# A two-layer encoder with a mixture of experts: the last tile's router products ahead of the other tiles' counts and gathers, and one copy of the gathered rows

## The chip, the cores and the metric

The kernel runs on one core of a Trainium2 chip. The time is the device time of one execution in microseconds (us), as a median of runs.

## What is computed

The reference is an encoder of two layers over 512 tokens of 1024 features in fp32. Each layer is a mixer (layer 0: retention and differential attention; layer 1: latent attention and gated linear attention), a residual and a layer norm, then a mixture of experts, another residual and another layer norm. The part that the change touches is the way from the mixer's output to the first expert, the router:

```python
grp_logits = xf @ w_grp + b_grp                 # 4 groups
g_idx = argmax(grp_logits)                      # top-1 group
exp_logits = (xf @ w_exp + b_exp).reshape(n, 4, 8)
in_grp = exp_logits of the chosen group         # 8 experts
top_l, top_e = lax.top_k(in_grp, 2)             # top-2 experts
gate = p_grp * softmax(top_l)
out = sum over the two experts e: gate * (silu(x @ w_gate[e]) * (x @ w_up[e])) @ w_down[e]
x = layer_norm(ALPHA * x + out)
```

There are 32 experts, each with three matrices of 2 MB, so a layer reads 201 MB of expert weights.

## The kernel before, in words

The 512 tokens are four tiles t = 0 to 3 of 128 rows. At the end of each layer's mixer, `out_rest` multiplies the last tiles by the output weights and routes all four. Its TensorE (PE) and VectorE (DVE) work runs in the order in which it is written, since `manual_schedule` names both engines there. ScalarE (ACT) and GpSimd (POOL) work is ordered by the scheduler.

The steps of a tile t are small helpers within `out_rest`:

- `total(t)` and `norm(t)`: the residual and the layer norm on DVE, and the tile's store to `x1d` in DRAM.
- `turn(t)`: eight 128x128 transposes on PE into PSUM, which two ACT copies bring to `mxT` (L1004).
- `logits(t)`: eight products of `mxT` with the 36 router columns.
- `choose(t)`: thirteen DVE steps that pick the group and the two experts, as closures in a list that `moe_choose` returns. The last one writes the 0/1 matrix `rab` (L1037).
- `count(t)`: 32-column products of `rab` with a triangle (`tri`) and, for the tiles ahead of it, with `ones`. They number the tokens of each expert. A tile's count needs the choices of all tiles up to it.
- `place(t)`: two DVE steps, `rpos` (L1048) and `S` (L1052). `S` is a 0/1 matrix that says which token goes to which of 64 places of the first experts.
- `gather(t)`: two products of 512 columns that add the rows of tile t, picked by `S`, to `m["g"]` in PSUM (tile name `pb`).

After the last tile, `moe_fit` finds out whether any expert has over 64 tokens and writes `rover`. All five engines then load `rover` (L1293), compare it and branch (L1294) over a slow general path that isn't taken here. In `moe`, the gathered rows `m["g"]` are copied to SBUF, one half by ACT and one by DVE (L1300). They are transposed on PE and copied by ACT (L1141), and the first expert's products `up(0, 0)` begin: 64 rows by 512 columns, in the rows `pa<-big 128*64 128x512`.

Expert weights come as 1 MB loads on SP's queue, in the order in which they are used. A load is issued as soon as a buffer slot is free, and slots come free as PE uses up earlier loads. SP takes the branch too, so loads that stand behind it in its queue wait for `rover`.

Of the kernel before, what the change touches and what calls it, by code (L numbers as in the profile page):

```python
# [77 lines left out]
class Kernel:  # L78
# [372 lines left out]
    def out_rest(self, pool, gbuf, m):  # L451

        nc = self.nc
        res = [self.residual(m, t) for t in range(NT)]
        first, last = self.order[:2], self.order[2:]
        ps, xT = {}, {}

        def begin(t):
            self.out_open(t)
            for q in first:  # L460
                self.out_mm(t, (2 * q, 2 * q + 1), q == first[0], False)

        def half_room():

            self.spare += 3
            for q in first:
                self.free(*self.out_w[q])
            self.free(*self.catbuf.pop(self.order[0] // 2))
            m.update(xbuf=self.slot(), xr=self.slot(), sc=self.slot(F32R))
            m["S"] = m["sc"][:, 0:D].rearrange("p (t e n) -> p t e n", t=NT, n=CAP)  # L470
            self.nc.gpsimd.memset(self.moe_fetched(m, 1), 0.0)
            self.spare -= 3
            self.pump()

        def out(t, *qs):
            for q in qs or last:
                if q not in self.out_w:
                    self.out_w[q] = self.next_w()
                self.out_mm(t, (2 * q, 2 * q + 1), False, q == last[-1])

        def room():

            for q in last:
                self.free(*self.out_w[q])
            self.free(*self.catbuf.popitem()[1])

        def total(t):

            tiles, halves = self.out_ps.pop(t)
            w = D // len(tiles)  # L490
            for i, z in enumerate(tiles):
                x = res[t][:, i * w:(i + 1) * w]
                nc.vector.scalar_tensor_tensor(x, x, ALPHA, z, op0=OP.mult, op1=OP.add)
            self.rel(*tiles)
            return self.ln_stats(pool, res[t])

        def norm(t, st):
            self.ln_apply(res[t], st, gbuf)
            nc.scalar.dma_start(self.x1d[t * P:(t + 1) * P, :], res[t])

        def turn(t):
            if t < 2:
                ps[t] = [self.pb()]
                halves = [ps[t][0][:, 0:512], ps[t][0][:, 512:D]]
            else:
                halves = ps[t] = [self.pa(), self.pa()]
            xT[t] = pool.tile([P, D], F32, name="mxT", bufs=3).rearrange("p (j n) -> p j n", j=KJ)
            self.moe_turn(m, xT[t], res[t], halves)

        def logits(t):  # L510

            z = ps[t]
            self.moe_logits(m, xT[t], z[0][:, 0:36])
            ps[t] = z, z[0][:, 0:36], (z[0][:, 512:D] if len(z) == 1 else z[1])[:, 0:NE]

        def choose(*ts):
            for steps in zip(*[self.moe_choose(m, pool, t, ps[t][1]) for t in ts]):
                for f in steps:
                    f()

        def count(t):
            self.moe_count(m, t, ps[t][2])

        def place(t, n=2):
            self.moe_place(m, t, ps[t][2], 2 * n)
            self.rel(*ps[t][0])

        def gather(t):

            if t == 0:  # L530
                m["g"] = self.pb()
            S = m["S"][:, t, 0:2].bitcast(F32).rearrange("p e n -> p (e n)")
            for hf in range(2):
                s = slice(hf * 512, (hf + 1) * 512)
                self.mm(m["g"][:, s], S, res[t][:, s], t == 0, t == NT - 1)

        while len(self.split_ready) < 2:
            self.prep_w()
        with self.tc.manual_schedule(engines={mybir.EngineType.PE, mybir.EngineType.DVE}):
            begin(2)  # L540
            begin(3)
            half_room()
            out(0)
            norm(0, total(0))
            out(1)
            norm(1, total(1))
            out(2)
            turn(0)
            norm(2, total(2))
            out(3, last[0])  # L550
            logits(0)
            choose(0)
            turn(1)
            out(3, last[1])
            room()
            count(0)
            st = total(3)
            place(0)
            logits(1)
            norm(3, st)  # L560
            turn(2)
            gather(0)
            logits(2)
            turn(3)
            choose(1, 2)
            count(1)
            place(1)
            logits(3)
            gather(1)
            count(2)  # L570
            place(2)
            choose(3)
            gather(2)
            count(3)
            place(3, 1)
            self.moe_fit(m)
            gather(3)
            self.moe_slots(m, 3, 2, 2)
# [623 lines left out]
    def moe(self, m, g, b):  # L1202

        nc, tc, l = self.nc, self.tc, m["layer"]
# [56 lines left out]
        def up(e, c):  # L1261
            if c == 0:
                acc[e] = self.pa()
            self.moe_up(acc[e], xn[:, e // 2 % 2, :, e % 2 * CAP:(e % 2 + 1) * CAP], c)
            if c == 1:
                h[e] = hh[64:128]
                self.moe_hidden(h[e], acc.pop(e))
# [27 lines left out]
            self.moe_general(m, r)  # L1295
        with tc.manual_schedule(engines={mybir.EngineType.PE}):
            x = self.moe_fetched(m, 0)
            for hf in range(2):
                s = slice(hf * 512, (hf + 1) * 512)
                (nc.scalar.copy, nc.vector.tensor_copy)[hf](x[:, s], m["g"][:, s])  # L1300
            self.rel(m.pop("g"))
            self.moe_features(x, xn[:, 0], 2)
            ps = self.pa()
            self.moe_tokens(m, m["S"][:, :, 2:4], self.idr, ps, 1)
            self.rel(ps)
            self.moe_fetch(m, 1, False)
            self.moe_gates(m)
            self.spare = 1
            up(0, 0)
            yhl = self.slot(F32R)  # L1310
            self.spare = 0
            up(0, 1)
            up(1, 0)
            for e in range(NE):
                q, k = divmod(e, 4)
                p = e // 2 - 1
                if e == NE - 10:
                    self.spare = 4
                if e == NE - 8:
                    last, cz, yz, gbuf = self.slot(local=False), self.slot(F32R, local=False), self.slot(F32R, local=False), None  # L1320
                    gbuf = self.load_gb(g, b)
                    self.spare = 0
                    nc.vector.tensor_copy(cz[:, T:T + P], self.eye)
                if e:
                    up(e, 1)
                    down(e - 1)
                    if e + 1 < NE:
                        up(e + 1, 0)
                if e == NE - 1:
                    hidden(e)  # L1330
                    break
                if e == 0:
                    features(1)
                    pair(0), pair(1)
                more = q + 1 < NE // 4
                if k % 2:
                    hidden(e)
                    if more and k == 1:
                        pair(2 * q + 3)
                    elif more:  # L1340
                        features(2 * q + 3)
                    continue
                add = 0 <= p < LAST - 1
                if add:
                    sums(p, 0)
                hidden(e)
                if add:
                    sums(p, 1)
                if more and k == 0:
                    pair(2 * q + 2)  # L1350
                elif more:
                    features(2 * q + 2)
                if add:
                    sums(p, 2, 3)
                if p == LAST - 2:
                    self.spare = 1
                    self.free(sc, yhl)
                    y = yz.rearrange("p (k n) -> p k n", k=2)
                    parts(0)
                    self.spare = 2  # L1360
                if e == NE - 2:
                    self.spare = 0
                    parts(1), parts(2)
            y1 = last[:, 0:D]
            sum_begin(0)
            down(NE - 1)
            sum_begin(1)
            for t in range(3):
                sum_end(t)
                if t == 0:  # L1370
                    sum_begin(2)
# [559 lines left out]
```

## Time and profile before

| | us |
|---|---|
| median of 3 runs (lowest, highest) | 1568.62 (1567.82, 1569.14) |
| the profiled execution: its time | 1568.2 |
| the profiled execution: its span, from the first to the last instruction | 1566.4 |
| PE busy | 1495.4 (95%) |
| DVE busy, ACT busy | 688.4 (44%), 441.1 (28%) |
| DMA queue of the weight loads | 69.8% of 16 engines' span |

PE is busy nearly everywhere, but not at one pace: the granted clock says in which stretches it ran at its lower level. Between the output products and the experts, PE, DVE and ACT hand small pieces to each other. There the timeline has to be read instruction by instruction.

### The profile page before, as it was taken

What the parts mean: (1) busy time and instruction counts of PE and PEld (TensorE: products, weight loads), DVE (VectorE), ACT (ScalarE), POOL (GpSimd) and SP (SyncE); (2) the same over time, 40 slices, a digit from 0 to 9 for tenths busy, and PEclk for the clock granted to TensorE, in tenths of its full rate; (3) what the DMA queues carried; (4) which work ended last, traced back from release to release, by engine and by line L of the source; (5) the groups of instructions that cost most, each with busy time, mean ns of one, the idle gap of its engine ahead of it and who ended that gap; (6) DMA issues with size and microseconds to landing.
All of it is one profiled execution on the core that took longest, in us unless ns stands there. A gap on an engine that the chain in (4) does not pass through costs nothing. (4 is left out here: it accounts for less than half of the span.)

```text
span 1566.4 us, 19698 instructions
## 1 busy us (share of the span) xinstructions
PE 1495.4 (95%) x7825; PEld 892.1 (57%) x7825; DVE 688.4 (44%) x1211; ACT 441.1 (28%) x772; POOL 185.7 (12%) x278
## 2 busy tenths in 40 slices
PE   7999999979999999999999899997999999999997
PEld 7888888844444444444358687675444444444433
DVE  4555655543334334343445634365333434334334
ACT  4545522012121121121235534512222122121222
POOL 3322211211000000010022200020100000001001
PEclk9999999989999999999999999999999999999998
DMA  8311133669999999999972111286999999999993
GB/s 239 109 54 54 55 108 134 243 236 393 425 426 426 426 427 425 426 426 426 427 260 97 54 54 55 79 340 261 401 426 427 425 427 427 425 426 425 427 427 127
DMA packets 106836, 465.11 MB, mean 297 GB/s; under 512 B 12972, under 2 KB 48268, under 8 KB 57456
## 3 DMA queue, kind: packets, MB, share of 16 engines
q1 hardware_dynamic: 98848, 444.86, 69.8%
q0 software_dynamic: 6160, 12.62, 2.3%
q10 hardware_dynamic: 1728, 6.29, 1.0%
q8 instruction: 63, 1.03, 0.2%
q14 instruction: 37, 0.30, 0.1%
HBM read 462.11 MB, written 9.44 MB: 301 GB/s over the span
## 5 line engine op out<-in xcount | busy, mean ns | idle before, releaser
L213 PE MATMUL pa<-big 128*64 128x512 f32 (+3 forms) x4168 | 831.0, 459 | 7.1 <-DMA big<-in_moe_w_up_dram 2.9
L213 PEld LDWEIGHTS pa<-big 128*128 128x128 f32 (+1 forms) x4168 | 449.5, 166 | 314.4 <-issue 268.1
L213 PE MATMUL pa<-big,hs 128*64 128x512 f32 x992 | 224.7, 592 | 0.0
L1198 DVE SCALAR_TENSOR_TENSOR big<-pa,rgate,big 64x512 fp32r<-64x512 f32 x120 | 90.0, 750 | 213.4 <-ACT big L1197 213.2
L213 PE MATMUL pb<-big 128*128 128x512 f32 (+1 forms) x544 | 160.3, 432 | 9.1 <-DVE big L1153 4.2
L1153 DVE SCALAR_TENSOR_TENSOR big<-big,pb 128x1024 f32<-128x1024 f32 x112 | 134.2, 1219 | 69.8 <-PE pb L213 69.5
L213 PEld LDWEIGHTS pa<-big,hs 128*64 128x64 f32 x992 | 72.9, 137 | 140.6 <-issue 136.0
L1197 ACT ACTIVATE big<-pa,rgate 64x512 fp32r<-64x512 f32 x120 | 81.8, 682 | 219.1 <-PE pa L213 170.3
L1168 DVE TENSOR_TENSOR h<-pa,h 64x512 f32<-64x512 f32 x64 | 44.5, 695 | 218.9 <-ACT h L1167 218.9
L213 PEld LDWEIGHTS pb<-big 128*128 128x128 f32 x544 | 98.0, 190 | 53.4 <-issue 25.2
L1167 ACT ACTIVATE h<-pa 64x512 f32<-64x512 f32 x64 | 37.6, 588 | 264.0 <-PE pa L213 264.0
L203 DVE TENSOR_TENSOR big<-big 128x2048 fp32r<-128x2048 f32 (+2 forms) x38 | 77.2, 2032 | 64.6 <-ACT big L203 46.6
L203 ACT CAST big<-big 128x2048 fp32r<-128x2048 f32 (+2 forms) x39 | 64.7, 1664 | 55.8 <-PE pa L213 22.8
L1130 POOL DMA_INDIRECT big<-x1d,ridx x30 | 31.4, 1045 | 355.0 <-DVE ridx L1104 243.0
L1141 ACT COPY big<-pb 128x1024 f32<-128x1024 f32 (+1 forms) x34 | 32.5, 962 | 121.0 <-PE pb L218 121.0
L1129 POOL MEMSET big<- 128x1024 f32 x28 | 26.6, 952 | 320.7 <-PE pb L218 315.1
L218 PEld LDWEIGHTS pa<-eye,h 64*128 64x128 f32 x256 | 35.4, 209 | 37.9 <-DVE big L1198 24.3
L213 PE MATMUL pb<-big,C 128*128 128x512 f32 x192 | 53.9, 412 | 2.5 <-DVE big L1153 2.5
L218 PE MATMUL pb<-eye,big 128*128 128x128 f32 x304 | 43.6, 286 | 10.5 <-DMA big<-in_x_dram 4.9
L218 PEld LDWEIGHTS pb<-eye,big 128*128 128x128 f32 x304 | 38.8, 194 | 17.4 <-issue 9.4
L1178 DVE COPY hs<-pa 128x256 f32<-128x256 f32 x64 | 26.9, 421 | 43.7 <-PE pa L218 43.6
L213 PEld LDWEIGHTS pb<-big,C 128*128 128x128 f32 x192 | 33.3, 188 | 19.4 <-issue 9.7
(314 smaller groups left out, 1200.1 us busy)
## 6 DMA issues: line engine op xcount, KB each, us to landing
big<-in_moe_w_gate_dram SPq DMA_DIRECT2D x128, 1024.0 KB, 19.5
big<-in_moe_w_up_dram SPq DMA_DIRECT2D x128, 1024.0 KB, 19.6
big<-in_moe_w_down_dram SPq DMA_DIRECT2D x128, 1024.0 KB, 19.6
big<-in_ev_w_in_dram SPq DMA_DIRECT2D x24, 512.0 KB, 5.3
big<-in_od_w_in_dram SPq DMA_DIRECT2D x7, 1024.0 KB, 5.8
big<-in_x_dram SPq DMA_DIRECT2D x8, 512.0 KB, 4.1
big<-in_ev_w_out_dram SPq DMA_DIRECT2D x4, 1024.0 KB, 4.8
x1d<-big ACTq DMA_DIRECT2D x8, 512.0 KB, 4.8
```

The lines of the kernel that those rows point to most:

```text
L203: ins = self.nc.scalar.copy(hi, src), (sub or self.nc.vector).tensor_tensor(lo, src, hi.bitcast(F32), op=OP.subtract)
L213: return self.nc.tensor.matmul(o, a, b, start=start, stop=stop, skip_group_check=True)
L218: self.nc.tensor.transpose(o, a, self.eye[s, s])
L1129: self.nc.gpsimd.memset(x, 0.0)
L1130: self.nc.gpsimd.indirect_dma_start(x, None, self.x1d[:, :], bass.IndirectOffsetOnAxis(m["idx"][:, pair:pair + 1], 0), bounds_check=T - 1, ...
L1141: self.nc.scalar.copy(xn[:, i * n:(i + 1) * n], ps[:, i * n * P:(i + 1) * n * P].rearrange("p (j n) -> p j n", j=n))
L1153: self.nc.vector.scalar_tensor_tensor(x, x, ALPHA if first else 1.0, ps, op0=OP.mult, op1=OP.add)
L1167: self.nc.scalar.activation(h, o[0:64], AF.Silu)
L1168: self.nc.vector.tensor_tensor(h, o[64:128], h, op=OP.mult)
L1178: self.nc.vector.tensor_copy(hs.rearrange("p j n -> p (j n)"), ps[:, 0:4 * CAP])
L1197: last = self.nc.scalar.activation(hi, src, AF.Copy, scale=g[a:a + 64])
L1198: self.nc.vector.scalar_tensor_tensor(yl[a:a + 64, s], src, g[a:a + 64], hi.bitcast(F32), op0=OP.mult, op1=OP.subtract)
```

## The change

Two functions change. In `out_rest`, `logits(1)` goes ahead of `count(0)`. `logits(3)` goes ahead of `count(1)`, right behind `turn(3)`. Both counts, of tiles 1 and 2, are written one behind the other. The list of thirteen steps of `choose(3)` is run step by step, and `place(1)` and `gather(1)` are put in ahead of its third step, `place(2)` and `gather(2)` ahead of its seventh. In `moe`, the copy of the gathered rows is one DVE copy of 128x1024 where it was an ACT copy and a DVE copy of 128x512 each.

```diff
             out(3, last[1])
             room()
+            logits(1)
             count(0)
             st = total(3)
             place(0)
-            logits(1)
             norm(3, st)
             turn(2)
             gather(0)
             logits(2)
             turn(3)
             choose(1, 2)
+            logits(3)
             count(1)
-            place(1)
-            logits(3)
-            gather(1)
             count(2)
-            place(2)
-            choose(3)
-            gather(2)
+            steps = self.moe_choose(m, pool, 3, ps[3][1])
+            for i, f in enumerate(steps):
+                if i in (2, 6):
+                    place(i // 4 + 1)
+                    gather(i // 4 + 1)
+                f()
             count(3)
             place(3, 1)
             self.moe_fit(m)
...
             x = self.moe_fetched(m, 0)
-            for hf in range(2):
-                s = slice(hf * 512, (hf + 1) * 512)
-                (nc.scalar.copy, nc.vector.tensor_copy)[hf](x[:, s], m["g"][:, s])
+            nc.vector.tensor_copy(x, m["g"])
             self.rel(m.pop("g"))
```

Line numbers behind the first hunk grow by one, so `rab` is written at L1038 in the changed kernel and the copy stands at L1299. No instruction but the copies is added or taken away, and SP's and POOL's instructions stand in the same order.

PE in layer 0, from `logits(2)` and `turn(3)` on, as a difference (`y_108` holds the router's weights):

```order
 L213 MATMUL pa<-y_108,mxT 128x36 x8
 L218 MATMUL pa<-eye,big 128x128 x8
+L213 MATMUL pa<-y_108,mxT 128x36 x8
 L213 LDWEIGHTS ones
 L213 MATMUL pb<-rab,ones 128x32
 L213 LDWEIGHTS tri
 L213 MATMUL pb<-rab,tri 128x32
-L213 MATMUL pa<-y_108,mxT 128x36 x8
-L213 MATMUL pb<-big 128x512 x2
 L213 LDWEIGHTS ones
 L213 MATMUL pa<-rab,ones 128x32
```

The products of `logits(3)` move ahead of tile 1's count, and `gather(1)` moves behind tile 2's count, where it stands next to `gather(2)`.

DVE in layer 0 before, from the last step of `choose(1, 2)` on:

```order
L1037 TENSOR_TENSOR rab<-y_108 128x32 x2
L1048 SCALAR_TENSOR_TENSOR rpos<-pb,rab 128x32
L1052 TENSOR_TENSOR big<-io,rpos 128x256
L1048 SCALAR_TENSOR_TENSOR rpos<-pa,rab 128x32
L1052 TENSOR_TENSOR big<-io,rpos 128x256
L1030 TENSOR_TENSOR y_108<-pa,y_108 128x36
L1024 TENSOR_REDUCE y_108<-y_108 128x1
```

The same place in the changed kernel:

```order
L1038 TENSOR_TENSOR rab<-y_108 128x32 x2
L1031 TENSOR_TENSOR y_108<-pa,y_108 128x36
L1025 TENSOR_REDUCE y_108<-y_108 128x1
L1049 SCALAR_TENSOR_TENSOR rpos<-pb,rab 128x32
L1053 TENSOR_TENSOR big<-io,rpos 128x256
L1026 SCALAR_TENSOR_TENSOR og,fm<-y_108,wt 128x4
L1027 TENSOR_SCALAR og<-og,fm 128x4
L1033 SCALAR_TENSOR_TENSOR s_2991<-og,y_108 128x32
L1025 TENSOR_REDUCE y_108<-s_2991 128x1
L1049 SCALAR_TENSOR_TENSOR rpos<-pa,rab 128x32
L1053 TENSOR_TENSOR big<-io,rpos 128x256
```

`choose(3)` begins right behind `rab` and has the two steps of `place(1)` and of `place(2)` within it, where both stood ahead of it.

DVE in layer 0 before, at the far end of the branch:

```order
L1294 UNCONDITIONAL_BRANCH x2
L1071 TENSOR_TENSOR y_108<-y_108 128x16
L1074 TENSOR_TENSOR y_108<-y_108 128x4
L1300 COPY big<-pb 128x512
L1073 TENSOR_REDUCE y_108<-y_108 128x4
```

DVE in the changed kernel, at the near end of the branch:

```order
L1065 TENSOR_SCALAR rkeep<-rkeep 128x1
L1053 TENSOR_TENSOR big<-io,rpos 128x128
L1299 COPY big<-pb 128x1024
L1294 TENSOR_LOAD rover
L1295 COMPARE_AND_BRANCH
```

DVE's copy now covers both halves and stands ahead of DVE's load of `rover`, where it stood behind the branch. In layer 1 DVE's rows move in the same way. ACT's copy is gone in both layers.

## Rows read from the trace of the kernel before

**Rows 1.** The page, 40 equal slices of the span: the granted clock in tenths.

```profile
PEclk9999999989999999999999999999999999999998
```

**Rows 2.** Stretches (us, each engine's busy time, granted clock, DMA share, GB/s), layer 0.

```profile
324.00:326.00 2.00, 0.12 (x2) 0.12 (x2) 1.96 (x19) 0.17 (x1) 0.00 (x0) 1.00 1.01 424
326.00:328.00 2.00, 2.00 (x12) 2.00 (x11) 0.61 (x2) 0.00 (x0) 0.00 (x0) 0.52 1.01 426
...
332.00:334.00 2.00, 1.18 (x6) 0.37 (x5) 0.82 (x4) 0.00 (x0) 0.00 (x0) 0.77 0.00 0
```

**Rows 3.** Timeline (start, us, engine, line, operation, [idle before <-releaser]), layer 0's router.

```profile
315.39 1.95 PE L213 MATMUL pb<-y,mxT 128*128 128x36 f32 x16
...
318.84 1.96 PE L213 MATMUL pb<-big 128*128 128x512 f32 x4 [0.56 <-DVE big L1052]
...
323.10 1.07 ACT L1004 COPY mxT<-pa 128x512 f32<-128x512 f32 x2 [4.14 <-PE pa L218]
...
325.65 0.31 DVE L1037 TENSOR_TENSOR rab<-y 128x32 bf16<-128x32 f32 x2
...
325.91 3.44 PE L213 MATMUL pa<-y,mxT 128*128 128x36 f32 x16
...
329.15 3.76 PE L213 MATMUL pb<-big 128*128 128x512 f32 x4
...
333.11 0.19 DVE L1048 SCALAR_TENSOR_TENSOR rpos<-pa,rab 128x32 f32<-128x32 f32 x1 [6.37 <-PE pa L213]
333.33 0.42 DVE L1052 TENSOR_TENSOR big<-io,rpos 128x256 fp32r<-128x256 f32 x1
333.68 0.19 DVE L1030 TENSOR_TENSOR y<-pa,y 128x36 f32<-128x36 f32 x1
...
333.81 1.98 PE L213 MATMUL pb<-big 128*128 128x512 f32 x4 [0.82 <-DVE big L1052]
...
335.64 0.23 PE L213 MATMUL pa<-rab,ones 128*128 128x32 bf16 x3
...
336.91 0.18 PE L213 MATMUL pa<-rab,tri 128*128 128x32 bf16 x1 [1.04 <-DVE rab L1037]
...
337.76 1.98 PE L213 MATMUL pb<-big 128*128 128x512 f32 x4 [0.58 <-DVE big L1052]
```

**Rows 4.** Timeline of layer 0, from the copy to the first expert, and SP's first load.

```profile
340.12 0.35 SPq L291 DMA_DIRECT2D big<-in_moe_w_gate_dram  x1
...
341.03 0.69 DVE L1300 COPY big<-pb 128x512 f32<-128x512 f32 x1 [1.32 <-ACT big L1300]
```

**Rows 5.** Timeline of layer 1, the same two places.

```profile
1070.66 0.32 DVE L1037 TENSOR_TENSOR rab<-y 128x32 bf16<-128x32 f32 x2
...
1082.46 1.98 PE L213 MATMUL pb<-big 128*128 128x512 f32 x4 [0.58 <-DVE big L1052]
...
1084.48 0.58 ACT L1300 COPY big<-pb 128x512 f32<-128x512 f32 x1 [15.29 <-PE pb L213]
...
1085.31 0.68 DVE L1300 COPY big<-pb 128x512 f32<-128x512 f32 x1
```

**Rows 6.** The page, costliest groups (count | busy, mean ns of one | idle before): a large PSUM read.

```profile
L1153 DVE SCALAR_TENSOR_TENSOR big<-big,pb 128x1024 f32<-128x1024 f32 x112 | 134.2, 1219 | 69.8 <-PE pb L213 69.5
```

**Rows 7.** Branch lines L1293, L1294: durations (ns min/median/max), first and last start (us).

```profile
L1293 DVEq TENSOR_LOAD <-rover x2: 319/434/548, 338.0 to 1082.7; - x2
...
L1294 DVEq EVENT_SEMAPHORE  x2: 21/21/21, 339.3 to 1083.7; - x2
```

**Rows 8.** PE's timeline: each layer's first expert products, and a later wait for weights.

```profile
343.68 11.97 PE L213 MATMUL pa<-big 128*64 128x512 f32 x48 [0.29 <-ACT big L1141]
...
781.85 3.65 PE L213 MATMUL pa<-big 128*64 128x512 f32 x14 [1.43 <-DMA big<-in_moe_w_up_dram]
...
1087.93 10.70 PE L213 MATMUL pa<-big 128*64 128x512 f32 x48 [0.33 <-ACT big L1141]
...
1524.20 3.65 PE L213 MATMUL pa<-big 128*64 128x512 f32 x14 [1.43 <-DMA big<-in_moe_w_up_dram]
```

## Prediction

> **What bounds the kernel now.** I read the page's row of the granted clock first: PE is at full clock nearly everywhere and has a dip in one of the 40 slices [rows 1]. That slice holds layer 0's router. Next come the stretches: from 324 to 326 us PE is busy for 0.12 of 2 us, while DVE is busy for 1.96 us with the choices of tiles 1 and 2. The weight stream still moves 424 GB/s. In the next stretch the granted clock is 0.52, and at 332 to 334 us the stream moves 0 GB/s [rows 2]. So the loads issued earlier have filled their slots, and nothing flows until PE uses some up. The router is therefore a serial piece in which neither PE nor the weight stream gets on. What shortens it should move both to the left.
>
> The timeline shows what it is made of, in layer 0 [rows 3]. DVE ends `rab` of tiles 1 and 2 at 325.96. Then PE does `logits(3)` in 3.44 us and `gather(1)` in 3.76 us, both at the lower clock level (1.2 GHz): the like products `logits(1)` took 1.95 us and `gather(2)` 1.98 us at the upper one (2.4 GHz). DVE waits 6.37 us for tile 2's count behind them and only then begins `choose(3)`. The count of tile 3 runs at 336.91 and `gather(3)` at 337.76. It ends at T = 339.74, and `up(0, 0)` begins at 343.68 [rows 8], that is T + 3.94. In layer 1 T is 1082.46 + 1.98 = 1084.44 [rows 5] and `up(0, 0)` begins at 1087.93 [rows 8], T + 3.49.
>
> **The change part by part.** First, `logits(1)` ahead of `count(0)`. It moves into PE's idle time ahead of `rab` of tile 0, and DVE takes `count(0)` up only behind `total(3)`. I cost it at nothing. If DVE were to wait for it, the cost would be at most the 1.95 us of the product [rows 3].
>
> Second, `logits(3)` behind `turn(3)`. ACT's two copies of tile 3 run from 323.10 to 324.17 [rows 3]. If the products can start behind the first copy they end at 323.65 + 1.95 = 325.6, and if they wait for both, at 326.1. DVE is free at 325.96, so `choose(3)` begins at 325.97 to 326.2. I take 326.07.
>
> DVE's chain then goes on without a pause. Adding the bias and the first maximum take 0.41 us (0.22 for the step behind 333.68 and 0.19 for the next). `place(1)` takes 333.68 - 333.11 = 0.57 us, so S of tile 1 starts at 326.07 + 0.41 + 0.22 = 326.70. PE follows the start of S by 333.81 - 333.33 = 0.48, so `gather(1)` starts at 327.18. A gather holds PE for 335.64 - 333.81 = 1.83 us [rows 3]. `choose(3)` and its two inserts are DVE work of 336.91 - 333.68 = 3.23 us (with the way to PE) and 2 x 0.57, so `rab` of tile 3 reaches PE at 326.07 + 3.23 + 1.14 = 330.44. PE gets there later: `gather(1)` and `gather(2)` end at 327.18 + 2 x 1.83 = 330.84, and the count of tile 3 follows at about 330.9 instead of 336.91. That is **6.0 us** in layer 0. S of tile 2 is ready before `gather(1)` ends, so the two run on.
>
> Layer 1 has the same rows 1070.66 - 325.65 = 745.01 us later [rows 3, 5]. From the count of tile 3 to the end of `gather(3)` the rows take 339.74 - 336.91 = 2.83 us, so T becomes 330.9 + 2.83 = 333.73 in layer 0 and 1078.74 in layer 1. The latter is 1084.44 - 1078.74 = **5.7 us** earlier.
>
> Third, the copy. A DVE copy of 128x1024 out of PSUM is not in the trace. One half took 0.69 us [rows 4], two of them 1.38, and DVE's steps of 128x1024 with one operand in PSUM 1.22 us each [rows 6]. I take 1.22, the nearest in shape, with 0.69 and 1.38 as ends. Before, the halves did not overlap: in layer 1 ACT copied from 1084.48 to 1085.06 and DVE from 1085.31 to 1085.99; in layer 0 DVE waited 1.32 us for ACT and ended at 341.72 [rows 4, 5]. From there to `up(0, 0)` it is 1.96 us in layer 0 and 1.94 us in layer 1 [rows 8]. Afterwards it is T + 0.04 + 1.22 + 1.95 = T + 3.21. So the copy gives 0.73 us in layer 0 and 0.28 us in layer 1, **1.0 us** in all; with the ends of its price, 2.1 or 0.7 us.
>
> A rule of the Trainium skill speaks against this edit. "Advanced Engine Details and Errata", Bank Collisions, says that ScalarE and VectorE can read PSUM at the same time at full bandwidth in different banks. The rows show the two halves one after the other, in both layers. By the rule the split copy could end at about T + 0.73, so giving it up would cost some 0.5 us a layer; by the rows it was not getting that, and the sum goes by the rows.
>
> What waits behind the copy: it stands ahead of DVE's load of `rover`, and it waits for `gather(3)`. DVE's branch work is queued behind it. From the start of that load to DVE's signal behind the branch it takes 339.3 - 338.0 = 1.3 us in layer 0 and 1.0 us in layer 1 [rows 7]. I let it run beside the copy, since DVE's sequencer, and not its datapath, does it: cost nothing. If it only began when the copy has ended, PE's transposes would come 1.0 to 1.3 us later in each layer. The gate weights behind it are needed well after the first products.
>
> Fourth, the clock behind the router. In layer 0 the first 48 products of the experts took 11.97 us against 10.70 in layer 1, so part of them ran at the lower level [rows 8]. From `up(0, 0)` to the wait at the stage's end it is 781.85 - 343.68 = 438.17 us in layer 0 and 1524.20 - 1087.93 = 436.27 in layer 1. One layer of two lost 1.9 us. The stretches there, transposes and small products, stay as they were, so I expect one in two again: nothing. The ends are 1.9 us gained (neither layer) and 1.9 us lost (both).
>
> **Does it reach the end?** In both layers PE waits 1.43 us for a weight load at the stage's end [rows 8], so the stream sets that end as much as PE does. But the stream stands still in the router [rows 2]. SP issues its first load there at 340.12, behind the branch [rows 4]; all further ones wait for slots that PE frees from `up(0, 0)` on. All of this moves with T, and the pause that is left is still a pause: the first load moves from 340.12 to about 334, and the stream was at 0 by 332.
>
> **The sum.** 6.0 + 5.7 + 1.0 = 12.7 us. The profiled execution took 1568.2 us, which is 0.4 us below the median; taken from the median, 1568.6 - 12.7 = **1555.9 us**. Runs that differ by 0.2%, 3.1 us, are about what a measurement of this kernel can tell from no change.
>
> **The rivals.**
>
> *The clock falls all the same.* PE still has gaps here, between `logits(3)` and `gather(1)`, and its small products may not hold the clock. For it: the level fell before 326 to 328 us, behind a stretch with 0.12 us of PE work [rows 2]. Against it: that place now holds `logits(3)`. Earlier in the router `logits(1)` and the transposes of `turn(2)` stand alike ahead of a gather, and `gather(0)`, at 318.84, took 1.96 us: the clock had not fallen [rows 3]. A gather at the lower level costs 3.76 - 1.98 = 1.78 us. One or both in each layer is 3.6 to 7.1 us: 1559.5 to 1563. Chance 0.16. The Trainium skill, "TensorE: Matmul & The Clock Gate", Part 4, says that transposes don't count as busy in the same way; the fall to 0.52 came behind the transposes of `turn(3)` and a pause, with which it agrees, and by it `logits(3)` alone has to hold the clock.
>
> *The branch queues behind the copy.* By the third part 1.3 + 1.0 = 2.3 us: 1558.2. For it: the load of `rover` is behind the copy on DVE. Against it: in layer 1 ACT had the same order, copy and then branch, and all was over soon after its copy. Chance 0.10.
>
> *The weight stream takes it back.* If the stage's end were set by a stream that doesn't start earlier, the time would stay at 1568. For it: PE's wait at the end of both stages. Against it: 0 GB/s at 332 to 334 us. Chance 0.07.
>
> *Slower.* The first expert products follow a pause of about 3.2 us, with transposes alone, at another moment than before. If the clock fell there in both layers and stayed low for more than the first products, the price decides: 48 of them take 10.70 us at the upper level and twice that at the lower one. All of them at the lower level in both layers would be 21.4 us against a gain of 12.7: 1577. The sign turns from 6.4 us a layer on. No fall in the rows lasted that long: the first 48 products of layer 0 lost 1.27 us. Chance 0.03.
>
> My forecast has 0.64. Its own range, with the ends of the copy and of the clock, is 1553 to 1558. The range takes in the branch rival and most of the clock rival: **1552.5 to 1562**. Faster has 0.64 + 0.16 + 0.10 = 0.90, the same 0.07, slower 0.03.
>
> **What would show it.** Right: `logits(3)` at about 1.95 us directly behind ACT's copies; the two gathers one behind the other, each under 2 us; the count of tile 3 some 5 us behind `rab` of tile 2 instead of 11; `up(0, 0)` 3.2 us behind `gather(3)`; a DVE copy of 1.2 us. Wrong: gathers near 3.8 us, a pause between the copy's end and the transposes of more than 0.2 us, or a longer wait for weights at the end of either stage, which would mean that the stream did not move with the router.

## The result and the profile after

The changed kernel takes 1561.82 us (median of 6 runs, 1560.17 to 1563.07), the kernel before 1568.88 (6 runs, 1567.02 to 1569.82). The ratio is 0.9946, with a 95% interval of 0.9935 to 0.9957. That is 7.1 us faster, where 12.7 was forecast. The time lies within the stated range and above the forecast's own range of 1553 to 1558. It is what the rival *the clock falls all the same* would give (1559.5 to 1563), so the range holds by that rival's price and not by the forecast. One of the runs below, the second of *after_again*, took 1704.17 us at a mean granted clock of 0.845; no ratio uses it.

The profiled execution took 1560.17 us, with a span of 1558.4 where it was 1566.4: 8.0 us. The chain of layer 0's router, from the timeline (start, us, engine, line, operation, [idle before <-releaser]); it answers to [rows 3, 4]:

```profile
318.46 1.96 PE L213 MATMUL pb<-big 128*128 128x512 f32 x4 [1.56 <-DVE big L1053]
...
322.72 1.07 ACT L1005 COPY mxT<-pa 128x512 f32<-128x512 f32 x2 [5.15 <-PE pa L218]
...
323.36 1.98 PE L213 MATMUL pa<-y,mxT 128*128 128x36 f32 x16 [0.28 <-ACT mxT L1005]
...
325.27 0.32 DVE L1038 TENSOR_TENSOR rab<-y 128x32 bf16<-128x32 f32 x2
325.51 0.19 DVE L1031 TENSOR_TENSOR y<-pa,y 128x36 f32<-128x36 f32 x1
...
326.50 5.40 PE L213 MATMUL pb<-big 128*128 128x512 f32 x8 [0.68 <-DVE big L1053]
...
329.36 0.19 DVE L1038 TENSOR_TENSOR rab<-y 128x32 bf16<-128x32 f32 x1
...
331.81 0.18 PE L213 MATMUL pa<-rab,tri 128*128 128x32 bf16 x1
...
332.10 0.19 DVE L1049 SCALAR_TENSOR_TENSOR rpos<-pa,rab 128x32 f32<-128x32 f32 x1 [2.55 <-PE pa L213]
...
332.67 1.98 PE L213 MATMUL pb<-big 128*128 128x512 f32 x4 [0.59 <-DVE big L1053]
...
334.70 1.23 DVE L1299 COPY big<-pb 128x1024 f32<-128x1024 f32 x1 [1.40 <-PE pb L213]
335.03 0.35 SPq L291 DMA_DIRECT2D big<-in_moe_w_gate_dram  x1
336.13 1.14 PE L218 MATMUL pb<-eye,big 128*128 128x128 f32 x8 [1.47 <-DVEq L1295]
...
337.94 10.59 PE L213 MATMUL pa<-big 128*64 128x512 f32 x48 [0.33 <-ACT big L1142]
```

Read it from the top. `logits(3)` follows ACT's first copy and takes 1.98 us, as forecast. `choose(3)` begins at 325.51, where it began at 333.68. But `gather(1)` and `gather(2)`, now one row, take 5.40 us instead of 3.66. DVE has `rab` of tile 3 at 329.55, and its count on PE must wait for the gathers until 331.81. DVE itself then waits 2.55 us for that count. The stretches (columns as in [rows 2]) show why:

```profile
324.00:326.00 2.00, 1.66 (x17) 1.42 (x16) 1.95 (x17) 0.00 (x0) 0.00 (x0) 1.00 1.03 430
326.00:328.00 2.00, 1.50 (x3) 0.75 (x4) 1.84 (x10) 0.00 (x0) 0.00 (x0) 0.78 0.99 416
328.00:330.00 2.00, 2.00 (x4) 0.80 (x3) 1.34 (x9) 0.00 (x0) 0.30 (x1) 0.50 1.04 436
```

PE's empty stretch at 324 to 326 us is gone (1.66 us busy instead of 0.12), and the granted clock still goes from 1.00 to 0.50, a little later. The lower level now falls on the two gathers, where it fell on `logits(3)` and `gather(1)`. Layer 1, from the same timeline, is worse:

```profile
1056.79 1.96 PE L213 MATMUL pb<-big 128*128 128x512 f32 x4 [1.64 <-DVE big L1053]
...
1061.68 1.98 PE L213 MATMUL pa<-y,mxT 128*128 128x36 f32 x16 [0.29 <-ACT mxT L1005]
...
1065.18 6.68 PE L213 MATMUL pb<-big 128*128 128x512 f32 x8 [0.68 <-DVE big L1053]
...
1072.08 0.19 DVE L1049 SCALAR_TENSOR_TENSOR rpos<-pa,rab 128x32 f32<-128x32 f32 x1 [3.84 <-PE pa L213]
...
1074.67 1.22 DVE L1299 COPY big<-pb 128x1024 f32<-128x1024 f32 x1 [1.40 <-PE pb L213]
...
1077.91 12.35 PE L213 MATMUL pa<-big 128*64 128x512 f32 x48 [0.33 <-ACT big L1142]
```

The two gathers take 6.68 us and DVE waits 3.84 for the count behind them. Here the first 48 expert products also ran partly at the lower level: 12.35 us, where layer 0 has 10.59. In the kernel before it was the other way round [rows 8].

PE's waits for weights at the two stages' ends are 1.42 and 1.71 us, against 1.43 and 1.43 before [rows 8]. So the stream took back 0.3 us in layer 1 at most:

```profile
773.84 3.65 PE L213 MATMUL pa<-big 128*64 128x512 f32 x14 [1.42 <-DMA big<-in_moe_w_up_dram]
...
1516.17 3.65 PE L213 MATMUL pa<-big 128*64 128x512 f32 x14 [1.71 <-DMA big<-in_moe_w_up_dram]
```

The program can be cut at four rows of PE's timeline in each layer: the end of the mixer's last products (`pa<-big 128*128 128x512 ... x12`), T, the start of `up(0, 0)`, and the wait for weights near the stage's end. The differences, in us, for all profiles of this study ("router" is from the mixer's end to T; layer 0 / layer 1; T is the end of `gather(3)`, as in the prediction):

| profile | gather(0) | gather(1), gather(2) | router | T to up(0, 0) | from up(0, 0) to that wait | span |
|---|---|---|---|---|---|---|
| before | 1.96 / 1.96 | 3.76, 1.98 / 3.30, 1.98 | 25.15 / 24.91 | 3.94 / 3.49 | 438.17 / 436.27 | 1566.4 |
| after | 1.96 / 1.96 | 5.40 / 6.68 | 20.44 / 22.18 | 3.29 / 3.27 | 435.90 / 438.26 | 1558.4 |
| order_only | 3.75 / 3.38 | 5.19 / 5.32 | 25.58 / 22.25 | 3.85 / 3.57 | 436.70 / 436.59 | 1563.2 |
| copy_only | 1.95 / 1.95 | 3.25, 1.98 / 3.76, 1.98 | 24.81 / 24.87 | 3.20 / 3.27 | 435.84 / 435.49 | 1563.3 |
| fill_router | 3.32 / 3.38 | 3.70 / 5.32 | 20.42 / 22.22 | 3.26 / 3.27 | 436.81 / 436.57 | 1558.1 |
| fill_tail | 1.95 / 3.41 | 3.70 / 5.34 | 18.74 / 22.27 | 3.27 / 3.26 | 436.94 / 436.36 | 1556.0 |
| before_fill | 1.96 / 1.95 | 1.96, 1.98 / 1.96, 1.99 | 21.90 / 21.97 | 4.34 / 3.51 | 439.14 / 434.82 | 1561.9 |
| after_again | 1.95 / 3.37 | 5.40 / 5.32 | 20.45 / 22.21 | 3.26 / 3.28 | 438.55 / 436.44 | 1559.1 |
| swap | 1.96 / 1.96 | 3.70 / 5.28 | 17.73 / 19.40 | 3.28 / 3.27 | 435.81 / 436.69 | 1551.4 |
| swap_fill | 1.96 / 1.96 | 3.70 / 3.70 | 17.75 / 17.82 | 3.28 / 3.27 | 435.82 / 436.31 | 1550.7 |
| sf_split | 1.96 / 1.96 | 3.70 / 3.70 | 17.74 / 17.82 | 3.86 / 3.59 | 437.00 / 435.69 | 1550.1 |
| swap_router | 1.96 / 1.96 | 3.70 / 3.70 | 17.74 / 17.82 | 3.27 / 3.26 | 435.88 / 438.23 | 1551.9 |

From before to after the routers gave 25.15 - 20.44 = 4.7 and 24.91 - 22.18 = 2.7 us, and the way from T to `up(0, 0)` 0.65 and 0.22. The expert stages gave 2.3 in layer 0 and took 2.0 in layer 1. The mixers and the program's end, which the change doesn't touch, took 0.6. Together that is 8.0.

### The profile page after: what moved, and what is told of

It is laid out like the page before. It is cut to its first block, busy times and chain, and to the rows that moved or that the text cites. A ratio compares the mean times of both kernels' runs of the same rounds, so it can differ in the third digit from the quotient of the medians.

```text
span 1558.4 us, 19694 instructions
## 1 busy us (share of the span) xinstructions
PE 1492.4 (96%) x7825; PEld 889.1 (57%) x7825; DVE 689.1 (44%) x1211; ACT 439.8 (28%) x770; POOL 185.7 (12%) x278
```

## The experiments

The theory was: the new order works as forecast, but the clock falls in the router all the same and costs what is missing. Its rivals: the order or the copy was worth less, or one of them lost something elsewhere.

**The two parts alone.** *order_only* is the changed kernel with the split copy put back:

```diff
-            nc.vector.tensor_copy(x, m["g"])
+            for hf in range(2):
+                s = slice(hf * 512, (hf + 1) * 512)
+                (nc.scalar.copy, nc.vector.tensor_copy)[hf](x[:, s], m["g"][:, s])
```

> The changed order, with the copy of the gathered rows in two halves by ScalarE and VectorE as before. Clock theory (what is missing of the forecast went into TensorE's lower clock level, and the copy did what was forecast, 0.65 us in layer 0 and 0.22 us in layer 1): 0.9 us slower than the changed kernel, so 6 us faster than before. Rival (the copy in front of VectorE's branch costs time that the trace hides): as fast as the changed kernel or up to 2 us faster.

Measured: 1562.16 us (median of 6, 1556.04 to 1564.95), ratio 0.9941 (0.9924 to 0.9958). The runs spread over 9 us, and they do so with the mean granted clock of the execution: the two at 0.992 took 1556.0 and 1557.5 us, the four at 0.985 to 0.987 took 1561.2 to 1565.0. In its profile (1564.95) layer 0's clock fell earlier than in the changed kernel, at `gather(0)`:

```profile
318.87 3.75 PE L213 MATMUL pb<-big 128*128 128x512 f32 x4 [1.56 <-DVE big L1053]
322.42 3.47 PE L213 MATMUL pa<-y,mxT 128*128 128x36 f32 x16
...
327.51 3.63 PE L213 MATMUL pa<-y,mxT 128*128 128x36 f32 x16
...
332.25 5.19 PE L213 MATMUL pb<-big 128*128 128x512 f32 x8 [0.97 <-DVE big L1053]
```

So the same order, with the same 1.56 us of waiting ahead of `gather(0)`, gave a router of 25.58 us in this layer of this execution and 20.44 in that of the changed kernel. The order doesn't fix the level. By its ratio *order_only* can't be told from the changed kernel (0.9946), so its time decides neither for the theory nor for the rival.

*copy_only* is the kernel before with the single DVE copy (the reverse of the diff above).

> The order of before, with the one VectorE copy. Clock theory: 0.9 us faster than before, with the first expert products 3.2 to 3.3 us behind the end of the last gather instead of 3.94 and 3.49 us. Rival (the copy in front of the branch costs): not faster than before, up to 2 us slower.

Measured: 1565.56 us (12 runs, 1564.04 to 1571.17), ratio 0.9981 (0.9971 to 0.9991), beside 1569.66 for the kernel before. By its profile the way from T to `up(0, 0)` became 0.74 and 0.22 us shorter, which is the forecast's 0.73 and 0.28. The other 2 to 3 us are not in rows that the copy touches. The expert stages are 2.3 and 0.8 us shorter than in the profile of before, the routers 0.4 together, and a mixer is 1.1 longer. The first 48 products of layer 0 took 10.59 us instead of 11.97. The stretches say what those 2.3 us of layer 0 are. Before, the granted clock fell twice behind the router:

```profile
343.00:347.00 4.00, 3.71 (x15) 1.71 (x15) 1.17 (x4) 2.66 (x4) 3.76 (x4) 0.57 0.55 196
360.00:364.00 4.00, 4.00 (x16) 1.66 (x16) 1.59 (x6) 0.58 (x1) 1.11 (x1) 0.57 1.00 419
```

In *copy_only* it did not:

```profile
343.00:347.00 4.00, 4.00 (x20) 2.04 (x21) 0.58 (x2) 1.89 (x3) 3.82 (x6) 1.00 0.63 204
360.00:364.00 4.00, 4.00 (x22) 1.43 (x20) 0.69 (x1) 0.59 (x1) 0.40 (x1) 1.00 1.00 416
```

The runs on record go the same way: the mean granted clock is 0.988 over the 12 runs of *copy_only* and 0.986 over the 17 of the kernel before on that chip.

**Unread products that keep PE busy.** Both kernels add to the changed one products whose sums are overwritten before anything reads them. *fill_router* has two in the router:

```diff
             choose(1, 2)
+            fill(ps[2][0][1], 256)
             logits(3)
             count(1)
             count(2)
+            fill(ps[3][0][1], 384)
```

> The changed kernel with two more products of the gather's kind in TensorE's pauses of the router, whose results nobody reads: 256 columns ahead of logits(3), 384 columns between count(2) and gather(1). Clock theory: the clock holds, gather(1) and gather(2) take 3.7 us together instead of 5.4 and 6.7 us, the last gather ends 1.5 to 3 us earlier in each layer, and the time is 3 to 5 us under the changed kernel's. Rival (the weight stream takes it back): the last gather ends earlier, the wait for weights at each stage's end grows by as much, and the time stays. If the fillers are too small to hold the clock: gathers as in the changed kernel, 0.3 us lost in each layer.

*fill_tail* has one behind `gather(3)`, in the wait for the copy and the branch:

```diff
             gather(3)
+            z = self.pa()
+            fill(z, 512)
+            self.rel(z)
             self.moe_slots(m, 3, 2, 2)
```

> The changed kernel with one more product of the gather's kind (512 columns, result unread) behind gather(3), while VectorE copies the gathered rows. Clock theory: the copy hides it, the first 48 expert products take 10.6 to 10.7 us in both layers instead of 10.6 and 12.35 us, and the time is 0 to 2 us under the changed kernel's. Rival (TensorE's branch waits for the filler): the first expert products begin 0.3 us and more later than 3.3 us behind gather(3), and the time is the same or up to 1 us over.

Measured, on the same chip as the two above: *fill_router* 1557.55 us (5 runs, 1555.59 to 1559.85), ratio 0.9919 (0.9907 to 0.9932); *fill_tail* 1559.73 (6 runs, 1557.81 to 1563.84), ratio 0.9943 (0.9928 to 0.9958), which can't be told from the changed kernel. The first agrees with the theory in its time, but its one profile doesn't show the reason that was expected (*fill_tail*'s expectation, a filler that the wait hides and first products at 10.6 to 10.7 us, is met). Its layer 0 has the gathers at the upper level behind the fillers, yet so has *fill_tail*, which has no filler there. The clock had already fallen and come back in the one and had not fallen in the other:

```profile
319.82 3.32 PE L213 MATMUL pb<-big 128*128 128x512 f32 x4 [1.56 <-DVE big L1060]
...
329.53 3.70 PE L213 MATMUL pb<-big 128*128 128x512 f32 x8
```

That is *fill_router*, and this is *fill_tail*:

```profile
319.59 1.95 PE L213 MATMUL pb<-big 128*128 128x512 f32 x4 [1.57 <-DVE big L1061]
...
327.62 3.70 PE L213 MATMUL pb<-big 128*128 128x512 f32 x8 [0.68 <-DVE big L1061]
```

In layer 1 both have `gather(0)` at 3.38 to 3.41 us and the later gathers at 5.32 to 5.34. So in *fill_router* the gathers ran partly low with a filler directly ahead of them: filling those two pauses alone did not keep the level. What *fill_tail* does give is the price of the order with no fall at all: a router of 18.74 us, with no filler in it.

**The clock without the order.** *before_fill* leaves the kernel before as it was and puts two unread products of 512 columns into PE's pause ahead of tile 1's count:

```diff
             choose(1, 2)
+            fill(ps[2][0][1], 512)
+            fill(ps[2][0][1], 512)
             count(1)
```

> The kernel before with nothing moved, and two unread products of 512 columns (about 1.95 us) in the pause of 2.4 us in which PE waits for the choices of tiles 1 and 2; what they write is overwritten. Theory (what PE does ahead of a stretch sets its clock level, and the level is a large part of what the router costs): logits(3) goes from 3.44 and 3.60 us to 1.98 and gather(1) from 3.76 and 3.30 to about 1.96, so up to 3 us in each layer, and the time comes out near 1563, ratio about 0.996, with no order changed. Rival (the order alone makes the gain): the two products only fill a wait, the gathers stay as they are, ratio 0.999 to 1.001. A third possibility is that the level falls at another place of the same router, with a ratio of 0.998.

Measured: 1563.72 us (6 runs, 1562.93 to 1568.90) beside 1572.32 for the kernel before, ratio 0.9959 (0.9942 to 0.9975), as the theory said. PE in layer 0's router:

```profile
323.74 1.88 PE L213 MATMUL pa<-big 128*128 128x512 f32 x4
...
326.34 0.18 PE L213 MATMUL pb<-rab,tri 128*128 128x32 bf16 x1 [0.70 <-DVE rab L1044]
326.37 1.95 PE L213 MATMUL pa<-y,mxT 128*128 128x36 f32 x16
328.15 1.96 PE L213 MATMUL pb<-big 128*128 128x512 f32 x4
```

The first row is the filler. Behind it `logits(3)` takes 1.95 us instead of 3.44 and `gather(1)` 1.96 instead of 3.76 [rows 3]. In layer 1 it is the same, 1.95 and 1.96 instead of 3.60 and 3.30. The routers are 3.2 and 2.9 us shorter though nothing in them was moved: the work that nobody reads costs nothing there, and the level is worth 3 us a layer. In layer 0 the clock fell later instead, and the first 48 expert products took 13.11 us (10.69 in layer 1), so part of the gain went there in this execution.

**The changed kernel again.** *after_again* is it, on the chip of the kernels around it.

> The changed kernel as it is, on the same chip as its variants. By its own six runs it should come out at a ratio of about 0.9946 (0.9935 to 0.9957). If the level of the clock in its router differs from one execution to the next, this profile shows the gathers of tiles 1 and 2 at 3.70 us in one layer or in both, where the first one showed 5.40 and 6.68; if what the order does to the clock is fixed, it shows the same two numbers again.

Measured: 1560.79 us (6 runs), ratio 0.9930 (0.9915 to 0.9944). Layer 0 repeats its 5.40 us. In layer 1 the clock falls at another place than in the first profile:

```profile
1059.23 3.37 PE L213 MATMUL pb<-big 128*128 128x512 f32 x4 [1.64 <-DVE big L1053]
...
1069.03 5.32 PE L213 MATMUL pb<-big 128*128 128x512 f32 x8 [0.68 <-DVE big L1053]
```

It falls ahead of `gather(0)`, comes back for the two sets of logits, and falls once more. The router takes 22.21 us, as with the single long fall (22.18). So the place of the fall isn't fixed, but the later gathers ran at 3.70 us in neither layer, which the expectation of a changing level had asked for.

**The pause ahead of gather(0).** In every profile with the changed order PE waits 1.56 to 1.66 us for `S` of tile 0, behind the transposes of `turn(2)`, where it waited 0.56 before [rows 3]. In 6 of the 10 routers with that order `gather(0)` ran below the upper level. *swap* lets `logits(2)` run in that pause:

```diff
             turn(2)
-            gather(0)
             logits(2)
+            gather(0)
             turn(3)
```

> The changed kernel with logits(2) ahead of gather(0), so that PE has no pause of 1.56 us (1.64 in layer 1) ahead of gather(0), and the joint choice of tiles 1 and 2 on DVE need not wait 1.22 us for logits(2). By the order alone: rab about 1.2 us earlier in each layer, so 2 to 2.5 us below the changed kernel, a ratio of about 0.993. If that pause is also what lets the clock fall in the router, gather(0) and the gathers of tiles 1 and 2 run at the upper level (1.96 and 3.70 us) in both layers, and the ratio comes to 0.990 to 0.992. If something else is late there (the copies of tile 2 on ACT, the norm of tile 3 that turn(3) needs), nothing is gained: 0.9945.

*swap_fill* has the same swap and all three unread products.

> The same with the three unread products of the two earlier kernels (256 columns ahead of logits(3), 384 between count(2) and gather(1), 512 behind gather(3)). They add some 0.6 us of PE to each layer's router where it doesn't all lie in pauses. Clock theory: both layers' gathers at the upper level in most executions, ratio 0.989 to 0.991, the lowest of all kernels. Rival (the fillers bring nothing once the pause is gone): the same as without them, or up to 1.2 us longer.

Measured: *swap* 1555.16 us (4 runs, 1553.20 to 1558.73), ratio 0.9903 (0.9885 to 0.9922); *swap_fill* 1550.76 (4 runs, 1549.47 to 1552.48), ratio 0.9865 (0.9848 to 0.9882). The second is the best kernel here, 10.0 us below the changed one on the same chip (1560.79). PE in layer 1, *swap* first:

```profile
1052.77 1.98 PE L213 MATMUL pa<-y,mxT 128*128 128x36 f32 x16 [0.24 <-ACT mxT L1005]
1054.58 1.96 PE L213 MATMUL pb<-big 128*128 128x512 f32 x4
...
1061.20 5.28 PE L213 MATMUL pb<-big 128*128 128x512 f32 x8 [0.97 <-DVE big L1053]
```

and *swap_fill*:

```profile
1053.95 1.98 PE L213 MATMUL pa<-y,mxT 128*128 128x36 f32 x16 [0.24 <-ACT mxT L1015]
1055.76 1.96 PE L213 MATMUL pb<-big 128*128 128x512 f32 x4
...
1062.37 3.70 PE L213 MATMUL pb<-big 128*128 128x512 f32 x8 [0.22 <-DVE big L1063]
```

The pause ahead of `gather(0)` is gone in both, and `gather(0)` is at the upper level in all 8 routers with the swap. It was so too in all 6 routers with the old order, where that pause was 0.54 to 0.56 us. A pause of 0.97 us ahead of the later gathers is left, and in *swap* they still ran low in one layer. With the fillers 0.22 us of it are left, and the gathers run at 3.70 in both layers, as in the other two kernels with the swap and those fillers (6 routers of 6). The mean granted clock of every run agrees: 0.988 to 0.989 in the changed kernel on this chip, 0.988 to 0.992 in *swap*, 0.994 to 0.995 in *swap_fill*. By the order alone the swap gives 18.74 - 17.73 = 1.0 us in layer 0, a little under the 1.2 expected.

**Which filler, and the copy once more.** *swap_router* takes the filler behind `gather(3)` out of *swap_fill* (the reverse of the diff of *fill_tail*).

> The same kernel with the single copy but without the unread product behind gather(3), so that only the two fillers ahead of logits(3) and of gather(1) are left. Theory (what PE does ahead of the gathers sets their level): both layers' gathers of tiles 1 and 2 at 3.70 us as with all three fillers, ratio 0.986 to 0.988. Rival (the filler behind gather(3), which covers the wait for the branch, is what brought the 4 us against the kernel with the swap alone): gathers as in that one (5.28 us in layer 1), ratio about 0.990.

*sf_split* is *swap_fill* with the split copy (the diff of *order_only*).

> The kernel with logits(2) ahead of gather(0) and the three unread products, with the copy of the gathered rows split over ACT and DVE again as in the kernel before. In that kernel both routers ran at the upper level, so the copy can be priced with little else that changes. By the rows of the profiles (from the end of gather(3) to the first expert products 3.94 and 3.49 us with the split copy, 3.28 and 3.27 with the single one) it should be 0.7 + 0.2 = 0.9 us longer: ratio about 0.987, where the single copy gave 0.9865. Rival (the single copy also keeps the clock up in the first expert products, since in copy_only it brought 3 to 4 us and not 1): 2 to 4 us longer, a ratio of 0.988 to 0.989, with the first 48 expert products of a layer above 10.7 us.

Measured, on one chip: *swap_router* 1553.00 us (4 runs, 1551.78 to 1554.65), ratio 0.9895 (0.9877 to 0.9913); *sf_split* 1551.82 (4 runs, 1550.96 to 1551.91), ratio 0.9886 (0.9870 to 0.9903). The kernel before took 1569.38 there. In *swap_router* the gathers are at 3.70 us in both layers, so the two fillers in the router do that without the third. Its ratio, though, is above the theory's 0.986 to 0.988 and beside the rival's 0.990, and can't be told from *swap* (0.9903) or from *swap_fill*; its profile has 12.39 us for the first 48 products of layer 1. Without the filler behind `gather(3)` those products ran partly low in 5 of 18 layers of these profiles, with it in none of 6. That is too few to call it shown. A fall a little later comes with it too: in *fill_tail* the granted clock is 0.58 at 352 to 356 us.

*sf_split* prices the copy with both routers alike: from T to `up(0, 0)` 3.86 - 3.28 = 0.58 and 3.59 - 3.27 = 0.32 us, 0.9 in all. The first 48 products are the same as with the single copy (10.59 and 10.70 us), so they give the rival, that the single copy keeps the clock up there, no support. But the ratio is 0.0021 above *swap_fill*'s, that is 3.3 us, as the rival had it, on another chip and with intervals that overlap. So the rival is not excluded. The halves stand one behind the other again:

```profile
332.19 0.58 ACT L1311 COPY big<-pb 128x512 f32<-128x512 f32 x1 [9.15 <-PE pb L213]
332.81 0.69 DVE L1311 COPY big<-pb 128x512 f32<-128x512 f32 x1 [2.02 <-ACT big L1311]
```

Whether the copy causes the other 2 to 3 us of *copy_only* stays open. They go with the granted clock behind the router, as shown above, and an expert stage's length also moves by 2 us between profiles of unchanged code (435.90 and 438.55 in the two profiles of the changed kernel).

## Why the prediction was off

**What bounds the router, and that it reaches the end: right.** The router's gain came through to the end of the program. SP's first load moved from 340.12 to 335.03, and the waits at the stages' ends grew by 0.3 us at most. The rival of the weight stream is out. One reading was short: the page's row has two slices below 9, not one; the last is at the program's end, and layer 1's fall doesn't show in it.

**`logits(1)` at nothing, `logits(3)` behind ACT's copies: right for the chain.** `gather(0)` starts 4.25 us behind the mixer's end, before and after. (What the move of `logits(1)` did to PE's pauses comes below.) `logits(3)` took 1.98 us, and `choose(3)` began at 325.51, a little ahead of the 326.07 of the sum.

**The copy: right in size, for another reason.** The single copy takes 1.23 and 1.22 us. The gain is 0.65 + 0.22 = 0.87 us in the profiles, and 0.9 with the routers alike, where the sum had 1.0. The transposes start 336.13 - 335.93 = 0.2 us behind the copy's end, so the branch ran beside it and its rival is out. But what released them is DVE's branch (`<-DVEq L1295`), and not the copy. DVE's load of `rover`, in the changed kernel and in *sf_split* (durations in ns, first and last start in us):

```profile
L1294 DVEq TENSOR_LOAD <-rover x2: 316/434/552, 334.7 to 1074.7; - x2
```

```profile
L1304 DVEq TENSOR_LOAD <-rover x2: 316/431/546, 332.8 to 1069.3; - x2
```

In both kernels it starts when DVE's copy starts, and the transposes follow 1.4 us later (334.7 to 336.13, 332.8 to 334.20). In *sf_split* the split copy's fault is that DVE's half, and the branch queued behind it, wait for ACT's half (332.19 to 332.77). Of copying itself the two halves have no more than the one. In the kernel before DVE took the branch first, and layer 0 lost its time elsewhere:

```profile
339.12 1.28 ACT L1300 ACT_TABLE_LOAD   x1 [14.95 <-ACTq L1294]
340.41 0.58 ACT L1300 COPY big<-pb 128x512 f32<-128x512 f32 x1
```

ACT's half stood behind this table load and began at T + 0.67, where layer 1's began at T + 0.04 [rows 5]. That is why the single copy gave more in layer 0; the sum had the amount from the rows without naming it.

**The term of the order: this step failed.** The sum put both gathers at 1.83 us each, at the upper level, and got 6.0 + 5.7 = 11.7 us. The routers gave 4.7 + 2.7 = 7.4. That is 4.3 of the 4.7 us that the spans fall short of the forecast. The runs show two things in that term which the sum did not keep apart:

- What the order gives if the level is the same. With no fall, the old order takes 21.90 us (*before_fill*) and the new one 18.74 (*fill_tail*): 3.2 us.
- What the level gives. In the old order, 25.15 - 21.90 = 3.2 us and 24.91 - 21.97 = 2.9.

So the forecast's 6.0 us of layer 0 was half order and half clock, and the clock half rested on the argument that the place of the low stretch now holds `logits(3)`. That did not hold. In the changed kernel the gathers lost 5.40 - 3.70 = 1.70 us in layer 0 (18.74 + 1.70 = 20.44, the router as measured) and 6.68 - 3.70 = 2.98 us in layer 1. The rival's own price, 1.78 us for a gather, was about right, and its 0.16 was too little.

The argument that kept it low was that `gather(0)` stood behind transposes and had not fallen. It was taken from a router in which PE waited 0.56 us there (0.55 in layer 1). The change itself made that wait 1.56 and 1.64 us (`logits(1)`, now ahead of `count(0)`, no longer stands between that count and the gather), and then `gather(0)` fell too, in 6 routers of 10; with the wait at 0.54 to 0.56 us it fell in none of 6, and with the swap in none of 8. Taking the pauses out of the same router brought it from 20.44 and 22.18 us to 17.75 and 17.82, of which about 1 us a layer is the order of the swap. Why a fall comes in one execution and not in the next stays open. The Trainium skill, "TensorE: Matmul & The Clock Gate", section "A second HAM failure mode: psum-queue depth-cycling", tells of another kernel in which PE was idle for short times between groups of products, often enough that the clock went up and down between its two levels. The runs here agree: in the changed kernel's routers PE has pauses of 0.6 to 1.7 us, and its gathers took 5.40 and 6.68 us where 3.70 is the upper level.

**The clock behind the router: right in sum, by luck.** Nothing was put down, with ends of 1.9 us to either side. The low first products went from layer 0 to layer 1, and the two expert stages together changed by 0.3 us. Which layer has them, and whether one has, differs from profile to profile (the table), and a second fall behind the first products (360 to 364 us before) was not read. The forecast *slower* needed far longer falls; none was seen (the longest first 48 products took 13.11 us, in *before_fill*).

## What to carry to other kernels

When a gain is read from a stretch at the lower clock level, split it: what the new order gives at one level for both kernels, and what the level gives. The second part is not sure as long as the new order leaves pauses among small products and transposes ahead of the dense ones. Moving a product out of one pause into another can open a new one, so list PE's waits after the change as well as those removed. An unread product in a pause that is there anyway is a cheap test of the second part, and can be a cure: in *before_fill* 1.9 us of them saved 3 us in each router, but in *fill_router* 1.5 us of them did not keep layer 1's gathers up.

## What the runs showed of the hardware

- The same program doesn't get the same clock twice. Between the two profiles of the changed kernel, `gather(0)` of layer 1 went from 1.96 to 3.37 us and the first 48 products of layer 0 from 10.59 to 12.12. In *order_only* runs of one program on one chip differ by 9 us, with mean granted clocks of 0.985 to 0.992.
- Behind pauses of 1.0 to 1.7 us among transposes and small products the granted clock went to its lower level (1.2 GHz) in some executions: `gather(0)` took 3.32 to 3.75 us instead of 1.96 in 6 of 10 routers with a pause of 1.56 to 1.66 us ahead of it, and in none of 14 with a shorter one or none. In the changed kernel `logits(3)`, sixteen records of 36 columns in a row, took 1.98 us itself, and part of the gathers behind it ran at the lower level (5.40 and 6.68 us instead of 3.70).
- Two halves of one copy out of PSUM, given to ACT and DVE, ran one behind the other in every profile that has them: 0.58 and 0.69 us, against 1.22 us for one copy. In *sf_split* DVE's half waited for ACT's, and DVE's load of `rover` for the branch, queued behind that half, began 0.6 us later than ACT's half (332.8 and 332.19).
